# TensorE in the order of the program's text from attention on, and P's key blocks transposed two ahead, in a hybrid encoder block

## The chip, the cores and the metric

The kernel is one launch on one core of a Trainium2 chip. The time is the device time of that launch in microseconds (us). The engines go by the names of the profile: PE (TensorE; PEld are its weight loads), DVE (VectorE), ACT (ScalarE), POOL (GpSimd), SP (it issues the DMAs here). Each engine works through a list of its own, in the order in which the built program has it; engines wait for one another by semaphores.

## The reference

One layer on x of 4096 tokens by 1024 channels, in float32:

```python
mod = c @ w_ada + b_ada;  shift, scale, gate = split(mod, 3)
h = rms_norm(x, norm_g) * (1 + scale) + shift
q, k, v, u, z = split(h @ w_in)              # 512, 512, 512, 512, 1024 columns
q, k = rms_norm per head of 64, with q_norm_g, k_norm_g
A = attention of 8 heads: each chunk of 64 tokens sees itself and the 8 chunks to its left,
    with a clipped relative bias, softmax in float32
Pl = trailing means over 2, 4, 8, 16 tokens minus the token, a linear map per group, a scale per channel
x = x + gate * ((concat(A, Pl) * silu(z)) @ w_out)
```

## The kernel before

Every float32 product is made of three (or two) matmuls of rounded parts: an operand is split into a high part (a cast, on ACT) and the remainder (a subtraction, on DVE or POOL). The helper `split` (L109) does that.

A first stage (to some 557 us) makes h, the gate z, the pooled half and sums of the weights, and puts them into DRAM. The change touches what follows it.

**Attention** goes in two phases of four heads. A phase has 8 sections of 512 tokens, and a section has one unit per head, so there are 64 units, counted 0 to 63. Per unit `u` three lists of small steps are merged evenly by their place in the list (`merge`, L41): `s2_items` of unit u, `s1_items` of unit u+1, and `work`.

- `s1_items` (L679): for each of four query blocks, the scores (`sps`, L697 and L698) go into one PSUM buffer. DVE adds the bias and takes the minimum (L702); ACT makes the exponential (L715) into a tile `p`.
- `s2_items` (L734): for each of up to eight key blocks j, in the order of `js`, `tr(j)` transposes P on PE (`ptps`, L745), ACT copies the high part (`pth`, L751), DVE makes the remainder (`ptl`, L752), and `pv` multiplies with V (`ops`, L763 and L764). `LOOK` says how many key blocks `tr` is ahead of `pv`. The first key block of the list, j = -1, reads the tiles `p` of all four query blocks. `fin` copies the unit's output on ACT (`osum`, L778) and adds on DVE (L779); in every second unit POOL multiplies it twice (L781, L782).
- `work` holds most often one block of `proj_items` (L589): the projection of 128 tokens to q, k (512 columns, 24 matmuls) and v (256 columns, 24 matmuls; L599 to L601), six blocks ahead of the unit at the start. q and k are copied by ACT (`qkr`, L612), squared by POOL (`sq`, L614) and summed by DVE (L621). After every second block an inverse square root is made of small steps: two on DVE (L95, L96) and thirteen on POOL (L94, L99 to L102); then POOL multiplies both blocks' `qkr` (L630). The halves of h come by DMA and are split by ACT (`bhh`, L110) and POOL (`bhl`, L111), in three buffers each.
- Into `work` go also the transposes of q and k (`tq_items`, L646; PE's L651), four per section. They read the normalised `qkr` of four blocks. The first of a section stands in the unit after the one in which its last block is projected.

Units 26 and 27 have no projection of the first phase left; the second phase's weights are loaded there. Units 58 to 62 have output blocks instead (`o_items`, L519): 512 columns, `ps` from a pool of two buffers, L528 to L530, emptied by ACT or by DVE (L540). The last stage (`d_items`) is output blocks alone.

What sets the order before: the program is written in one order, but a scheduler with a timeline of its own puts each engine's instructions into the order in which it takes them to be ready:

```python
    with tile.TileContext(nc, schedule_with_timeline_sim=True) as tc:
```

Of the kernel before, what the change touches and what calls it, by code (L numbers as in the profile page):

```python
# [20 lines left out]
P = 128  # L21
# [7 lines left out]
HD = 64  # L29
HP = 4  # L30
WIN = 640
LOOK = 1
NPAIR = 16
EPS = 1e-6
NEG = 1e30
# [16 lines left out]
def block_kernel(ctx, tc, x, xT, par, crow, w_adaT, w_in, w_uT, bias, w_pool, w_out, rcnt, out):  # L52
# [423 lines left out]
                    load_wqkv(0, 1, lambda: a_stage(), nc.vector)  # L476


    op = ctx.enter_context(tc.tile_pool(name="b_qk", bufs=9))
    WO = {}  # L480

# [37 lines left out]
    def o_items(i):  # L519
        half, p = osteps[i]  # L520

        def one(k):
            if half == 0 and k == 0:
                XP[p] = (pp.tile([P, SG], F32, name="ps"), load_xr(p, 0))
            ps, xr = XP[p]
            a_, l_ = OH[i]
            wh, wl = WO[10 * half][k]
            nc.tensor.matmul(ps, a_[:, k, :], wh, start=half == 0 and k == 0, stop=False, skip_group_check=True)  # L528
            nc.tensor.matmul(ps, a_[:, k, :], wl, start=False, stop=False, skip_group_check=True)
            nc.tensor.matmul(ps, l_[:, k, :], wh, start=False, stop=k == 3, skip_group_check=True)  # L530
            if k == 3:
                OH.pop(i)
                o_load(i + 2)
                o_done(i)
                if half == 0:
                    t = op.tile([P, 512], F32, name="qkr")
                    nc.scalar.copy(t, ps)
                    nc.sync.dma_start(s1_d[p], t)
                else:
                    nc.vector.tensor_tensor(xr, ps, xr, op=ALU.add)  # L540
                    nc.sync.dma_start(out[p * P : (p + 1) * P, 0:512], xr)
                    XP.pop(p)

        return [lambda k=k: one(k) for k in range(4)]

    with ExitStack() as cb:
# [42 lines left out]
        def proj_items(ph, b, after=None):  # L589
# [3 lines left out]
            def chunk(c, k):  # L593
                if k == 0:
                    hold[c] = pp.tile([P, SG], F32, name="ps")
                ps = hold[c][:, 0:512] if c == 0 else hold[c][:, 0:256]
                a_, l_ = hq[(ph, b), k]
                wh, wl = WB[ph, c, k]
                nc.tensor.matmul(ps, a_, wh, start=k == 0, stop=False)  # L599
                nc.tensor.matmul(ps, a_, wl, start=False, stop=False)  # L600
                nc.tensor.matmul(ps, l_, wh, start=False, stop=k == KT - 1)  # L601
                if k == KT - 1:
                    if c == 0:
                        evac_qk(ps)
                    else:
                        evac_v(ps)
                if c == 1 and k in (3, 7) and after is not None:
                    load_h(*after, k // 4, nc.vector if ph == 0 and b < 5 else None)
# [37 lines left out]
        def tq_items(ph, sg):  # L646
            def tq(which, pair):
                ps = ptp.tile([P, SG], F32, name="ptps")
                c0 = which * 256 + pair * P
                for i in range(NB):  # L650
                    nc.tensor.transpose(  # L651
                        out=ps[:, i * P : (i + 1) * P], in_=QK[ph, sg * NB + i][:, c0 : c0 + P], identity=ident
                    )
                for e in range(2):
# [24 lines left out]
        def s1_items(ph, sg, h):  # L679
            def one(i):  # L680
# [13 lines left out]
                ks = ring[h]  # L694
                for pos, k0, n in parts:
                    o = ps[:, pos : pos + n]
                    nc.tensor.matmul(o, QS[ph, sg, h][:, qc], ks[:, k0 : k0 + n], start=True, stop=False)  # L697
                    nc.tensor.matmul(o, QL[ph, sg, h][:, qc], ks[:, k0 : k0 + n], start=False, stop=True)  # L698
                w0 = 0 if sg > 0 else 512 - i * P
                p_ = sp.tile([P, WIN], F32, name="p")  # L700
                mx = st.tile([P, 1], F32, name="mx")
# [32 lines left out]
        def s2_items(ph, sg, h):  # L734
# [5 lines left out]
            def tr(j):  # L740
                ilo, ihi = max(j, 0), min(j + 4, 3)
                ps = ptp.tile([P, SG], F32, name="ptps")
                for i in range(ilo, ihi + 1):
                    w = (j - i + 4) * P
                    nc.tensor.transpose(  # L745
                        out=ps[:, i * P : (i + 1) * P], in_=Pt[ph, sg, h, i][:, w : w + P], identity=ident
                    )
                r = slice(ilo * P, (ihi + 1) * P)
                a_ = wk.tile([P, SG], F32R, name="pth", bufs=3)
                l_ = wk.tile([P, SG], F32R, name="ptl", bufs=3)  # L750
                nc.scalar.copy(a_[:, r], ps[:, r])  # L751
                nc.vector.tensor_tensor(l_[:, r], ps[:, r], a_[:, r].bitcast(F32), op=ALU.subtract)  # L752
                pts[j] = (a_, l_, r)

            def pv(n):
# [4 lines left out]
                a_, l_, r = pts.pop(j)  # L760
                v = Vt[ph, sg * NB + j][:, pr, e, :]
                last = n == len(js) - 1
                nc.tensor.matmul(o[:, r], v, a_[:, r], start=n == 0, stop=False, skip_group_check=True)  # L763
                nc.tensor.matmul(o[:, r], v, l_[:, r], start=False, stop=last, skip_group_check=True)  # L764
                if last:
                    fin(o)

# [76 lines left out]
        def d_items(i):  # L844
            t, p = steps[i]

            def one(k):
# [12 lines left out]
                a_, l_ = DH[t, p]  # L860
                wh, wl = WO[11 if t == 0 else t][k]
                start = t in (1, 2) and k == 0
                nc.tensor.matmul(ps, a_[:, k, :], wh, start=start, stop=False, skip_group_check=True)
                nc.tensor.matmul(ps, a_[:, k, :], wl, start=False, stop=False, skip_group_check=True)  # L864
                nc.tensor.matmul(ps, l_[:, k, :], wh, start=False, stop=k == 3, skip_group_check=True)  # L865
                if k < 3:
                    return

# [156 lines left out]
```

## Time and profile before

| | us |
|---|---|
| three runs | 1914.45, 1915.05, 1915.29 (median 1915.05) |
| the profiled execution, its span | 1916.19, 1914.3 |
| PE, PEld busy | 1876.1 (98%), 1616.1 |
| DVE, ACT, POOL busy | 1198.1, 914.9, 697.7 |

A line of the profile names the source line, the engine, the operation, and the tiles as out<-in, with buffer numbers left out. "Idle before" is the idle time of the engine right before such instructions, and what ended most of it. The end of a matmul is modelled, and matmuls overlap, so the distance from one start to the next says what a matmul takes from PE.

### The profile page before, as it was taken

The page shows a single profiled execution, that of the slowest core. Times are in us where ns is not written, and L with a number is a line of the kernel's source. Part 1 is how long each engine was busy: PE and PEld are TensorE (multiplying, and loading weights), DVE is VectorE, ACT ScalarE, POOL GpSimd, SP SyncE. Part 2 cuts the span into 40 slices and gives each one's busy share as a digit, 9 for nine tenths or more (in the row PEclk, how much of TensorE's full clock was granted, in tenths as well). Part 3 has the DMA queues.
Part 4 walks back from the last instruction along what each step waited for, and adds up shares of the span by engine and source line. Part 5 has one row for each costly group of instructions (what it writes and reads, how often), then busy time and mean ns, then how long its engine had stood idle before and what let it go on. Part 6 is the DMA issues. An engine that isn't in the chain of part 4 may idle for free.

```text
span 1914.3 us, 29736 instructions
## 1 busy us (share of the span) xinstructions
PE 1876.1 (98%) x10284; PEld 1616.1 (84%) x10284; DVE 1198.1 (63%) x2424; ACT 914.9 (48%) x1951; POOL 697.7 (36%) x966
## 2 busy tenths in 40 slices
PE   8999999999999999999999999999999999989999
PEld 7888888888888888888887888988988888878887
DVE  8676666575544457656656665576566555478875
ACT  5422223332324457656657665576566666432221
POOL 0421355244135553444454564534444433200000
PEclk8999999999999999999999999999999999999999
DMA  9566466567222222221223222222212457686662
GB/s 376 192 198 198 151 216 213 185 200 258 75 100 73 72 67 67 65 69 53 60 83 111 78 85 75 69 61 67 67 62 67 181 185 230 234 297 221 208 205 78
DMA packets 196727, 265.63 MB, mean 139 GB/s; under 512 B 21984, under 2 KB 98272, under 8 KB 196576
## 3 DMA queue, kind: packets, MB, share of 16 engines
q1 hardware_dynamic: 196576, 263.73, 42.1%
q8 instruction: 81, 1.33, 0.3%
q14 instruction: 70, 0.57, 0.1%
HBM read 177.54 MB, written 77.74 MB: 133 GB/s over the span
## 4 chain that ended last, share of the span: by engine, by line
PE 90%; DVE 4%; ACT 2%; DMA 2%; issue 1%; SPq 0%; POOL 0%; ACTq 0%; DVEq 0%; POOLq 0%
PE ps L599 9%; PE ps L600 9%; PE ps L601 9%; PE ptps L745 6%; PE aps L330 5%; PE aps L332 5%; PE aps L331 5%; PE ps L330 4%; PE ps L331 4%; PE ps L332 4%; PE sps L697 3%; PE ops L764 3%; PE sps L698 3%; PE ops L763 3%; PE ptps L865 2%; PE ptps L864 2%
## 5 line engine op out<-in xcount | busy, mean ns | idle before, releaser
L599 PE MATMUL ps<-w,bhh 128*128 128x512 f32 (+1 forms) x1024 | 353.9, 346 | 0.8 <-ACT bhh L110 0.8
L600 PE MATMUL ps<-w,bhh 128*128 128x512 f32 (+1 forms) x1024 | 352.3, 344 | 0.4 <-DVE w L111 0.4
L601 PE MATMUL ps<-w,bhl 128*128 128x512 f32 (+1 forms) x1024 | 351.0, 343 | 0.0
L752 DVE TENSOR_TENSOR ptl<-ptps,pth 128x512 fp32r<-128x512 f32 x480 | 223.4, 485 | 157.3 <-ACT pth L751 153.0
L702 DVE CUSTOM_DVE_ANT_0 p<-sps,nb 128x640 f32<-128x640 f32 (+4 forms) x256 | 199.0, 777 | 127.6 <-PE sps L698 126.5
L751 ACT CAST pth<-ptps 128x512 fp32r<-128x512 f32 x480 | 192.5, 425 | 147.1 <-PE ptps L745 123.1
L111 POOL TENSOR_TENSOR bhl<-bhr,bhh 128x512 fp32r<-128x512 f32 x148 | 190.8, 1292 | 157.7 <-ACT bhh L110 123.4
L715 ACT ACTIVATE p<-p,mx 128x640 f32<-128x640 f32 (+4 forms) x256 | 204.5, 799 | 91.0 <-DVE mx L702 88.5
L745 PE MATMUL ptps<-ident,p 128*128 128x128 f32 x1200 | 215.3, 275 | 1.6 <-ACT p L715 1.4
L599 PEld LDWEIGHTS ps<-w,bhh 128*128 128x128 f32 x1024 | 194.2, 190 | 19.0 <-DVE v L111 1.1
L600 PEld LDWEIGHTS ps<-w,bhh 128*128 128x128 f32 x1024 | 194.1, 190 | 18.5 <-DVE w L111 1.1
L601 PEld LDWEIGHTS ps<-w,bhl 128*128 128x128 f32 x1024 | 194.1, 190 | 16.4
L763 PE MATMUL ops<-pth,v 128*128 128x512 f32 x480 | 162.3, 339 | 5.7 <-ACT pth L751 3.5
L745 PEld LDWEIGHTS ptps<-ident,p 128*128 128x128 f32 x1200 | 147.4, 140 | 21.0 <-ACT p L715 1.9
L697 PE MATMUL sps<-kr,qs 128*128 128x320 f32 (+2 forms) x480 | 154.5, 330 | 8.8 <-DVE mx L702 7.3
L764 PE MATMUL ops<-ptl,v 128*128 128x512 f32 x480 | 154.2, 331 | 2.9 <-DVE ptl L752 2.2
L614 POOL TENSOR_TENSOR sq<-qkr 128x512 f32<-128x512 f32 x64 | 66.6, 1041 | 247.1 <-ACT qkr L612 238.6
L331 PE MATMUL aps<-hlo,w 128*128 128x512 f32 x392 | 152.8, 390 | 0.0
L332 PE MATMUL aps<-hhi,w 128*128 128x512 f32 x392 | 152.8, 390 | 0.0
L330 PE MATMUL aps<-hhi,w 128*128 128x512 f32 x392 | 149.6, 392 | 0.0
L698 PE MATMUL sps<-kr,ql 128*128 128x320 f32 (+2 forms) x480 | 147.3, 317 | 0.0
L331 PE MATMUL ps<-hlo,w 128*128 128x512 f32 x376 | 146.6, 390 | 0.0
(202 smaller groups left out, 3932.0 us busy)
## 6 DMA issues: line engine op xcount, KB each, us to landing
bhr<-hT_d SPq DMA_DIRECT2D x128, 256.0 KB
xt<-in_x_dram SPq DMA_DIRECT2D x32, 512.0 KB
qkr<-in_x_dram SPq DMA_DIRECT2D x64, 256.0 KB
out_dram<-qkr SPq DMA_DIRECT2D x64, 256.0 KB
yv<-yT_d SPq DMA_DIRECT2D x61, 256.0 KB
xt<-in_xT_dram SPq DMA_DIRECT2D x28, 512.0 KB
hT_d<-xt SPq DMA_DIRECT2D x56, 256.0 KB
w<-wg_d SPq DMA_DIRECT2D x20, 512.0 KB
```

The costliest lines, as they stand in the source:

```text
L330: nc.tensor.matmul(ps, wh[:, cs], a_, start=k == 0, stop=False)
L331: nc.tensor.matmul(ps, wh[:, cs], l_, start=False, stop=False)
L332: nc.tensor.matmul(ps, wl[:, cs], a_, start=False, stop=k == KT - 1)
L599: nc.tensor.matmul(ps, a_, wh, start=k == 0, stop=False)
L600: nc.tensor.matmul(ps, a_, wl, start=False, stop=False)
L601: nc.tensor.matmul(ps, l_, wh, start=False, stop=k == KT - 1)
L697: nc.tensor.matmul(o, QS[ph, sg, h][:, qc], ks[:, k0 : k0 + n], start=True, stop=False)
L698: nc.tensor.matmul(o, QL[ph, sg, h][:, qc], ks[:, k0 : k0 + n], start=False, stop=True)
L745: nc.tensor.transpose(out=ps[:, i * P : (i + 1) * P], in_=Pt[ph, sg, h, i][:, w : w + P], identity=ident)
L752: nc.vector.tensor_tensor(l_[:, r], ps[:, r], a_[:, r].bitcast(F32), op=ALU.subtract)
L763: nc.tensor.matmul(o[:, r], v, a_[:, r], start=n == 0, stop=False, skip_group_check=True)
L764: nc.tensor.matmul(o[:, r], v, l_[:, r], start=False, stop=last, skip_group_check=True)
```

## The change

Three things change. `LOOK` goes from 1 to 2. `pth` and `ptl` have four buffers instead of three. And every matmul and transpose from attention on goes through `mm` or `turn_`, which tie it behind the instruction that stands before it on PE in the text: PE's list from there on is the order of the text, whatever the scheduler takes to be ready. The other engines' lists are still the scheduler's, which makes them for this order of PE. In the changed kernel all these matmuls bear the helper's lines, L481 and L484, and lines behind the helpers are 7 higher (L751 is L758, L778 is L785, L630 is L637).

```diff
-LOOK = 1
+LOOK = 2
...
+    def mm(*a, **kw):
+        tc.keep_in_program_order(nc.tensor.matmul(*a, **kw))
+
+    def turn_(**kw):
+        tc.keep_in_program_order(nc.tensor.transpose(**kw))
...
 # o_items, output blocks (three matmuls; the same in proj_items and d_items)
-            nc.tensor.matmul(ps, a_[:, k, :], wh, start=half == 0 and k == 0, stop=False, skip_group_check=True)
+            mm(ps, a_[:, k, :], wh, start=half == 0 and k == 0, stop=False, skip_group_check=True)
...
 # tq_items, transposes of q and k
-                    nc.tensor.transpose(
+                    turn_(
                         out=ps[:, i * P : (i + 1) * P], in_=QK[ph, sg * NB + i][:, c0 : c0 + P], identity=ident
...
 # s1_items, scores
-                    nc.tensor.matmul(o, QS[ph, sg, h][:, qc], ks[:, k0 : k0 + n], start=True, stop=False)
-                    nc.tensor.matmul(o, QL[ph, sg, h][:, qc], ks[:, k0 : k0 + n], start=False, stop=True)
+                    mm(o, QS[ph, sg, h][:, qc], ks[:, k0 : k0 + n], start=True, stop=False)
+                    mm(o, QL[ph, sg, h][:, qc], ks[:, k0 : k0 + n], start=False, stop=True)
...
 # s2_items, transposes of P and products
-                    nc.tensor.transpose(
+                    turn_(
                         out=ps[:, i * P : (i + 1) * P], in_=Pt[ph, sg, h, i][:, w : w + P], identity=ident
                     )
                 r = slice(ilo * P, (ihi + 1) * P)
-                a_ = wk.tile([P, SG], F32R, name="pth", bufs=3)
-                l_ = wk.tile([P, SG], F32R, name="ptl", bufs=3)
+                a_ = wk.tile([P, SG], F32R, name="pth", bufs=4)
+                l_ = wk.tile([P, SG], F32R, name="ptl", bufs=4)
...
-                nc.tensor.matmul(o[:, r], v, a_[:, r], start=n == 0, stop=False, skip_group_check=True)
-                nc.tensor.matmul(o[:, r], v, l_[:, r], start=False, stop=last, skip_group_check=True)
+                mm(o[:, r], v, a_[:, r], start=n == 0, stop=False, skip_group_check=True)
+                mm(o[:, r], v, l_[:, r], start=False, stop=last, skip_group_check=True)
```

**First place: ACT, entering unit 21.** p_9774 is the exponential of the unit's last query block, osum_9795 the copy of the finished unit's output, ops its products. Before:

```order
L751 CAST pth_9697<-ptps_9693 128x384
L751 CAST pth_9718<-ptps_9716 128x128
L751 CAST pth_9742<-ptps_9739 128x256
L715 ACTIVATE p_9774,ls_9636<-p_9774,mx_9775 128x640
L612 COPY qkr_10355<-ps_10257 128x512
L751 CAST pth_9762<-ptps_9760 128x128
L751 CAST pth_9817<-ptps_9812 128x512
L751 CAST pth_9830<-ptps_9825 128x512
L110 CAST bhh_10471<-bhr_10469 128x512
L715 ACTIVATE p_9842,ls_9845<-p_9842,mx_9843 128x640
L778 COPY osum_9795<-ops_9641 64x512
```

After the change:

```order
L722 ACTIVATE p_9730,ls_9636<-p_9730,mx_9731 128x640
L110 CAST bhh_9808<-bhr_9806 128x512
L758 CAST pth_9757<-ptps_9755 128x128
L785 COPY osum_9795<-ops_9658 64x512
L722 ACTIVATE p_9774,ls_9636<-p_9774,mx_9775 128x640
L110 CAST bhh_9970<-bhr_9968 128x512
L110 CAST v_9801<-ps_9716 128x2x64
L758 CAST pth_9817<-ptps_9812 128x512
L110 CAST v_9801<-ps_9716 128x2x64
```

The copy of the output stood seven rows behind the exponential; now it stands right ahead of it.

**Second place: PE, at the first transposes of q and k for section 6** (ptps out of ident and qkr; qkr_9904 is the last of the section's four blocks, projected into ps_9821). Before:

```order
L745 MATMUL ptps_10042<-ident_178,p_9842 128x128
L745 MATMUL ptps_10042<-ident_178,p_9884 128x128
L745 MATMUL ptps_10042<-ident_178,p_9951 128x128
L651 MATMUL ptps_10067<-ident_178,qkr_9259 128x128
L651 MATMUL ptps_10067<-ident_178,qkr_9483 128x128
L651 MATMUL ptps_10067<-ident_178,qkr_9704 128x128
L651 MATMUL ptps_10067<-ident_178,qkr_9904 128x128
L601 MATMUL ps_10584<-w_4611,bhl_10472 128x256
L599 MATMUL ps_10584<-w_4611,bhh_10471 128x256
L600 MATMUL ps_10584<-w_4612,bhh_10471 128x256
L601 MATMUL ps_10584<-w_4611,bhl_10472 128x256
L599 MATMUL ps_10693<-w_4445,bhh_10623 128x512
```

After the change:

```order
L481 MATMUL ps_10026<-w_4455,bhh_9970 128x512
L481 MATMUL ps_10026<-w_4456,bhh_9970 128x512
L481 MATMUL ps_10026<-w_4455,bhl_9971 128x512
L484 MATMUL ptps_10064<-ident_178,p_9842 128x128
L484 MATMUL ptps_10064<-ident_178,p_9884 128x128
L484 MATMUL ptps_10064<-ident_178,p_9951 128x128
L484 MATMUL ptps_10072<-ident_178,qkr_9259 128x128
L484 MATMUL ptps_10072<-ident_178,qkr_9487 128x128
L484 MATMUL ptps_10072<-ident_178,qkr_9704 128x128
L484 MATMUL ptps_10072<-ident_178,qkr_9904 128x128
L481 MATMUL ops_10085<-pth_10035,v_8264 128x512
L481 MATMUL ops_10085<-ptl_10036,v_8264 128x512
```

The last projection matmul into ps_9821 stood 382 rows ahead of the row that reads qkr_9904, and stands 74 rows ahead of it now. p_9995, the last query block's P of the unit, was transposed 15 rows after the q and k blocks; now that is done before them.

**Third place: POOL, between sq_9906 and the normalised qkr_9904** (sq_9906 stands eight rows ahead of this piece before, and eight ahead after the change). Before:

```order
L100 TENSOR_TENSOR rqw_9911<-rqw_9911,rqv_9909 128x16
L101 TENSOR_SCALAR rqw_9911<-rqw_9911 128x16
L102 TENSOR_TENSOR rqy_9910<-rqw_9911,rqy_9910 128x16
L99 TENSOR_TENSOR rqw_9911<-rqy_9910 128x16
L100 TENSOR_TENSOR rqw_9911<-rqw_9911,rqv_9909 128x16
L111 TENSOR_TENSOR bhl_10188<-bhr_10185,bhh_10187 128x512
L101 TENSOR_SCALAR rqw_9911<-rqw_9911 128x16
L102 TENSOR_TENSOR rqy_9910<-rqw_9911,rqy_9910 128x16
L630 TENSOR_TENSOR qkr_9704<-qkr_9704,rqy_9910 128x512
L630 TENSOR_TENSOR qkr_9904<-qkr_9904,rqy_9910 128x512
L781 TENSOR_TENSOR osum_9359<-osum_9359,gzb_9508 128x512
L782 TENSOR_TENSOR osum_9359<-osum_9359,rlx_9349 128x512
```

After the change:

```order
L99 TENSOR_TENSOR rqw_9911<-rqy_9910 128x16
L788 TENSOR_TENSOR osum_9795<-osum_9795,gzb_9944 128x512
L100 TENSOR_TENSOR rqw_9911<-rqw_9911,rqv_9909 128x16
L789 TENSOR_TENSOR osum_9795<-osum_9795,rlx_9785 128x512
L101 TENSOR_SCALAR rqw_9911<-rqw_9911 128x16
L102 TENSOR_TENSOR rqy_9910<-rqw_9911,rqy_9910 128x16
L99 TENSOR_TENSOR rqw_9911<-rqy_9910 128x16
L100 TENSOR_TENSOR rqw_9911<-rqw_9911,rqv_9909 128x16
L101 TENSOR_SCALAR rqw_9911<-rqw_9911 128x16
L102 TENSOR_TENSOR rqy_9910<-rqw_9911,rqy_9910 128x16
L637 TENSOR_TENSOR qkr_9704<-qkr_9704,rqy_9910 128x512
L637 TENSOR_TENSOR qkr_9904<-qkr_9904,rqy_9910 128x512
```

Between sq_9906 and the two qkr stood two bhl and the thirteen small steps; now two bhl, the small steps and the two multiplications of osum_9795, the output of the unit that has just been finished.

## Rows read from the trace of the kernel before

**Rows 1.** Stage window of attention: us, busy us of each engine, clock, DMA.

```profile
557.00:1640.00 1083.00, 1065.65 (x6602) 942.80 (x6601) 647.27 (x1517) 660.83 (x1507) 507.42 (x785) 1.00 0.29 91
```

**Rows 2.** Groups of PE, 557 to 1640: count, busy, mean ns, idle before.

```profile
L599 PE MATMUL ps<-w,bhh 128*128 128x512 f32 (+1 forms) x1024 | 353.9, 346 | 0.8 <-ACT bhh L110 0.8
...
L745 PE MATMUL ptps<-ident,p 128*128 128x128 f32 x1142 | 204.9, 275 | 0.4 <-ACT p L715 0.2
L763 PE MATMUL ops<-pth,v 128*128 128x512 f32 x456 | 154.5, 339 | 5.1 <-ACT pth L751 2.9 <-DVE osum L779 0.4 <-DVE rt L721 0.4
L697 PE MATMUL sps<-kr,qs 128*128 128x320 f32 (+2 forms) x464 | 149.6, 331 | 8.8 <-DVE mx L702 7.3 <-DVE kr L671 0.3
...
L528 PE MATMUL ps<-w,bhh 128*128 128x512 f32 x98 | 39.3, 404 | 0.0
L651 PE MATMUL ptps<-ident,qkr 128*128 128x128 f32 x256 | 38.9, 273 | 0.0
```

**Rows 3.** Timeline of PE: start, duration, line, tiles, columns.

```profile
1104.15 0.39 PE L601 MATMUL ps<-w,bhl 128*128 128x512 f32 x1
1104.38 0.28 PE L599 MATMUL ps<-w,bhh 128*128 128x256 f32 x1
...
1105.35 1.04 PE L745 MATMUL ptps<-ident,p 128*128 128x128 f32 x8
```

**Rows 4.** Timeline: one score, its bias on DVE, its exponential on ACT.

```profile
1433.61 0.34 PE L698 MATMUL sps<-kr,ql 128*128 128x384 f32 x1
...
1433.78 0.28 PE L697 MATMUL sps<-kr,qs 128*128 128x256 f32 x1
...
1433.90 0.28 PE L698 MATMUL sps<-kr,ql 128*128 128x256 f32 x1
...
1434.22 0.82 DVE L702 CUSTOM_DVE_ANT_0 p<-sps,nb 128x640 f32<-128x640 f32 x1 [1.23 <-PE sps L698]
...
1435.09 0.83 ACT L715 ACTIVATE p<-p,mx 128x640 f32<-128x640 f32 x1 [1.23 <-DVE mx L702]
```

**Rows 5.** Groups of ACT, 557 to 1640.

```profile
L110 ACT CAST bhh<-bhr 128x512 fp32r<-128x512 f32 x151 | 93.3, 619 | 68.6 <-PE ps L600 25.6 <-issue 15.2 <-POOL bhl L111 8.3
...
L778 ACT COPY osum<-ops 64x512 f32<-64x512 f32 x60 | 34.8, 580 | 22.0 <-PE ops L764 20.3 <-issue 0.4 <-POOL qkr L630 0.2
L110 ACT CAST v<-ps 128x128 fp32r<-128x128 f32 x128 | 33.0, 263 | 11.5 <-DVE v L111 10.9
```

**Rows 6.** Timeline of POOL: a normalisation of q and k.

```profile
1215.86 1.04 POOL L614 TENSOR_TENSOR sq<-qkr 128x512 f32<-128x512 f32 x1 [7.88 <-ACT qkr L612]
1216.86 1.30 POOL L781 TENSOR_TENSOR osum<-osum,gzb 128x512 f32<-128x512 f32 x1
1218.13 1.29 POOL L111 TENSOR_TENSOR bhl<-bhr,bhh 128x512 fp32r<-128x512 f32 x1
...
1222.43 0.22 POOL L99 TENSOR_TENSOR rqw<-rqy 128x16 f32<-128x16 f32 x1
1222.72 0.22 POOL L100 TENSOR_TENSOR rqw<-rqw,rqv 128x16 f32<-128x16 f32 x1
...
1227.14 2.04 POOL L630 TENSOR_TENSOR qkr<-qkr,rqy 128x512 f32<-128x512 f32 x2
```

**Rows 7.** Groups of DVE, 557 to 1640.

```profile
L540 DVE TENSOR_TENSOR qkr<-ps,qkr 128x512 f32<-128x512 f32 x11 | 7.6, 688 | 3.1 <-PE ps L530 3.0
```

**Rows 8.** Stage window behind a long wait of PE.

```profile
1708.00:1711.50 3.50, 3.50 (x10) 2.72 (x9) 3.14 (x6) 0.00 (x0) 0.00 (x0) 0.51 1.04 355
```

**Rows 9.** Timeline of PE there: matmuls of 512 columns.

```profile
1707.59 0.50 PE L863 MATMUL ps<-w,bhh 128*128 128x512 f32 x1 [2.35 <-DVE qkr L870]
...
1708.22 0.63 PE L865 MATMUL ps<-w,bhl 128*128 128x512 f32 x1
...
1711.57 0.40 PE L864 MATMUL ps<-w,bhh 128*128 128x512 f32 x1
```

More of the change, by code (lines that the diff above doesn't have):

```diff
@@ L527, in one @@
             wh, wl = WO[10 * half][k]
-            nc.tensor.matmul(ps, a_[:, k, :], wh, start=half == 0 and k == 0, stop=False, skip_group_check=True)
-            nc.tensor.matmul(ps, a_[:, k, :], wl, start=False, stop=False, skip_group_check=True)
-            nc.tensor.matmul(ps, l_[:, k, :], wh, start=False, stop=k == 3, skip_group_check=True)
+            mm(ps, a_[:, k, :], wh, start=half == 0 and k == 0, stop=False, skip_group_check=True)
+            mm(ps, a_[:, k, :], wl, start=False, stop=False, skip_group_check=True)
+            mm(ps, l_[:, k, :], wh, start=False, stop=k == 3, skip_group_check=True)
             if k == 3:
@@ L598, in chunk @@
                 wh, wl = WB[ph, c, k]
-                nc.tensor.matmul(ps, a_, wh, start=k == 0, stop=False)
-                nc.tensor.matmul(ps, a_, wl, start=False, stop=False)
-                nc.tensor.matmul(ps, l_, wh, start=False, stop=k == KT - 1)
+                mm(ps, a_, wh, start=k == 0, stop=False)
+                mm(ps, a_, wl, start=False, stop=False)
+                mm(ps, l_, wh, start=False, stop=k == KT - 1)
                 if k == KT - 1:
@@ L862, in one @@
                 start = t in (1, 2) and k == 0
-                nc.tensor.matmul(ps, a_[:, k, :], wh, start=start, stop=False, skip_group_check=True)
-                nc.tensor.matmul(ps, a_[:, k, :], wl, start=False, stop=False, skip_group_check=True)
-                nc.tensor.matmul(ps, l_[:, k, :], wh, start=False, stop=k == 3, skip_group_check=True)
+                mm(ps, a_[:, k, :], wh, start=start, stop=False, skip_group_check=True)
+                mm(ps, a_[:, k, :], wl, start=False, stop=False, skip_group_check=True)
+                mm(ps, l_[:, k, :], wh, start=False, stop=k == 3, skip_group_check=True)
                 if k < 3:
```

## The prediction

> **What bounds the kernel now.** I read the stage windows first, then the groups of PE, then pieces of the timeline. From 557 to 1640 us, the attention stage with most of the output blocks, PE is busy for 1065.65 of 1083 us at full granted clock, and DVE, ACT and POOL for 661 at most [rows 1]. So PE sets the time there, and a change can win only what PE waits, and lose by whatever new wait it gives PE.
>
> How much PE waits is not the 17 us of idle time, because a matmul that waits behind its weights' load is shown as a longer one. I count starts instead: the next matmul starts 0.23 us after one of 512 columns, a transpose takes 0.11 in a row of eight [rows 3]; 384 columns take 0.17 and 256 take 0.12 [rows 4]; 320 and 128 lie at 0.147 and 0.06 by their columns. L599 to L601 run 1024 times each, half at 512 and half at 256 columns: 534 us. L745 1142 and L651 256 transposes: 152 us. L763 and L764, 911 in all over four widths, mean 0.146: 133 us. L697 and L698, 928, mean 0.146: 136 us. L528 to L530, some 292: 67 us [rows 2]. Together 1022 us of 1083: PE waits 61 us in this stage. The largest shares named are the score matmul L697 behind DVE's L702 and the products L763 behind ACT's copies [rows 2]. L651, the transposes of the normalised q and k, wait 0.0 [rows 2], because the projections run far ahead of them: 382 rows of PE's order stand between a block's projection and the first transpose that reads it.
>
> **The change, part by part.** (a) One tile more of pth and ptl, and transposes two ahead: nothing is added in work, the same 10,256 matmuls. A product now stands at least 2 us of PE work behind its transposes, over a copy and a subtraction, so the L763 and L764 waits go. (b) Score matmuls stand evenly, some 3.3 us apart, against the 1.1 us that DVE needs to empty their one buffer [rows 4]: the L697 waits go. I take all 61 us as removed. What PE waits after 1640 I leave as it is. What is late next is what was moved to get there.
>
> (c) The strict order brings the reader close behind its producer at three places.
>
> *Entering a unit.* The first key block's transposes read all four query blocks' P, the last of which was scored late in the unit before. In the odd units with a projection block PE has, between the end of that score and the transpose that needs it, 2 products of 256 and 2 of 128 columns, 6 projection matmuls of 256 and 3 transposes: 1.41 us. In the even ones three matmuls of 512 more: 2.09. The chain needs: DVE starts 0.2 after the matmul, 0.82 for L702, 0.83 for the exponential L715 right behind it [rows 4], 0.14 to PE: 2.0 at best. But ACT's order now puts the copy of the finished unit's output (L778, 0.58) ahead of that exponential (first place of the order above), and its products end 0.72 after the score: 0.72+0.2+0.58 [rows 5]+0.83+0.14 = 2.45. Wait 1.0 in the odd, 0.35 in the even units. Where a bhh cast (0.62) stands there too, 1.65; where it and a v cast (0.26) stand behind the end of a projection block, 0.96+0.2+0.62+0.26+0.83+0.14 = 3.0, wait 0.9 [rows 5]. By ACT's order: 16 units at 1.0, 7 at 1.65, 11 at 0.35, 12 at 0.9, and 8 early units of each phase at 1.0 to 1.25: 51 us. If ACT's order cost nothing, 0.6 in the odd ones alone: 15 us. Each wait holds everything on PE behind the transpose, projections included.
>
> *The q and k transposes, 15 times (sections 1 to 15).* In the second place of the order above, PE's row for qkr_9904 comes after the projection of that block by 74 rows: 9 matmuls of 512, 28 of 256, 12 of 320, 2 of 384, 4 of 128 and 18 transposes; with the projection's last matmul 10.0 us, with the unit's 0.9 above 10.9. The producer is POOL. Its order in the third place, counted from that matmul's start: copy done at 1.0, sq 1.04, two bhl at 1.29, thirteen small steps at 0.29, two osum at 1.3, two qkr at 1.02 [rows 6]: 13.0. Two waits inside it: the first bhl's cast stands on ACT behind the copies of the running products (about 1.5), and the first small step's seed stands on DVE behind L702 of the last score (about 1.1); handovers 0.4. In all 16.1, so PE waits 5.2; times 15, 78 us. Bounds: with none of the four big foreign steps and no waits the chain is 8.6, and PE waits nothing; the chain in rows 6, with two osum, two bhl and a second sq inside, takes 13.3 from sq's start, 14.3 in all, a wait of 3.4; one foreign step more makes 17.5 and 6.6. I take 5.2, nearest to the list as it stands.
>
> *The output blocks (units 58 to 62).* Block p+1 begins in the buffer that DVE empties for block p-1 right before: 0.2+0.69 [rows 7]+0.1 = 1.0, less up to 0.5 of attention between: 0.8 at 15 places, 12 us. Between 0, if the merge always puts attention there, and 15.
>
> At the change of phase (units 26 and 27) no projection stands between, and POOL splits the next weights: PE is at the q and k transposes sooner and the chain is longer. I count that place at two more such waits, 11 us, between 0 and 20.
>
> (d) The clock. After a wait of 2.35 us near 1707 the granted clock was at 0.51, the lower level of 1.2 GHz, from 1708.0 to 1711.5 [rows 8]; eight matmuls of 512 columns took 3.35 us there instead of 1.8, a loss of 1.5 [rows 9]. The 5.2 us waits lie well above 2.35, the unit waits below: 15 times 1.5 is 23 us; 0 if the clock stays up, 46 if it stays down twice as long. The Trainium skill, TensorE: Matmul & The Clock Gate, section "Why this matters for your kernels", speaks against the change here: it says to leave no idle gaps between bursts of matmuls, since one brings the clock back down. By it the whole 23 us stand, without it the sum is 23 less; rows 8 and 9 agree with it.
>
> Sum, against the profiled execution's own 1916.2 us (span 1914.3): -61 +51 +78 +12 +11 +23 = +114, 2030. The median of the runs shown lies 1.1 below that execution: 2029.
>
> **The rivals.** *Short chain.* POOL's chain comes out as in rows 6, 3.4 us each (51), and the clock falls at every second one (12): -61+51+51+12+11+12, 1992. For it: most of the 2.6 of inner waits is my hand count. Against: the order of POOL and DVE is fixed, and lists them. *The strict order only removes waits (the other side).* If POOL had q and k ready within 10.9, as its own pieces (8.6) would allow, and the exponentials came as soon as their scores allow, what is left is 15 at the units and 12 at the outputs: -61+27, 1882. It decides where the new waits stay under 61. For it: POOL is busy in under half of the stage [rows 1]. Against: osum and bhl stand inside the chain in its order, and rows 6 show them being run there. *Nothing changes.* If PE's order were already nearly the text's, 1915; the 382 rows against 74 speak against it. *The waits feed each other*: the 5.2 us hold back the projection whose half of h the next chain's bhl waits for, and the clock stays down longer: 15 times 8 instead of 5.2, and 23 more, some 2095.
>
> **How the numbers follow.** Forecast 0.73, its own range 1995 to 2080; short chain 0.14; longer waits 0.06; only removed 0.05; nothing 0.02. The time is 2029. The range of 1985 to 2075 holds nearly all of the first case and about half of the second. Two runs of this kernel that differ by less than 0.2% (4 us) can't be told apart: faster 0.05, same 0.02, slower 0.93.
>
> **What would show it.** In the profile after, the transposes of q and k (ptps out of ident and qkr) should show 15 waits on POOL's qkr, some 5 us each, where before they had 0.0; the transposes of p some 50 waits on ACT's exponential of 0.3 to 1.7; L697's and L763's successors nearly none; PE's clock should fall for some microseconds behind each long wait. PE's idle time from its first projection to its last transposes should be near 170 us. I am wrong if the q and k waits are under 2 us, or if PE waits for something that I don't list, a transfer above all.

## The result, and the profile after

The changed kernel takes 2066.54 us (median of 4 runs, 2066.14 to 2066.98), the one before, run beside it, 1915.17: a ratio of 1.0789, 95% interval 1.0776 to 1.0803. It is slower by 151 us, where 114 were forecast.

The page's busy times and the row of the granted clock come first; in the second each digit is one fortieth of the span.

```profile
span 2065.2 us, 29785 instructions
...
PE 1919.7 (93%) x10284; PEld 1640.2 (79%) x10284; DVE 1216.2 (59%) x2424; ACT 921.1 (45%) x1951; POOL 697.4 (34%) x966
...
PEclk9999999999999999999998999999999999999999
```

The same stage as [rows 1], which now ends near 1790:

```profile
557.00:1790.00 1233.00, 1106.87 (x6607) 965.08 (x6605) 668.90 (x1525) 669.86 (x1516) 502.91 (x784) 0.96 0.26 81
```

Nearly the same matmuls (6607 against 6602) take 1233 us instead of 1083. PE is idle for 126 us of them instead of 17, and the mean clock is 0.96 instead of 1.00, although the page's digits hardly show it. DVE, ACT and POOL do the same work as before: nothing was added, something is waited for. The groups of PE say what (now all of line 481 or 484, so they are told apart by their tiles; these answer to L745, L697, L763 and L651 in [rows 2], where all widths of a line stand together; here each width has a row of its own):

```profile
L484 PE MATMUL ptps<-ident,p 128*128 128x128 f32 x1153 | 219.3, 282 | 37.4 <-ACT p L722 36.0 <-DVE ptl L759 1.3
...
L481 PE MATMUL sps<-kr,qs 128*128 128x320 f32 x242 | 75.1, 318 | 0.0
L481 PE MATMUL ops<-pth,v 128*128 128x512 f32 x115 | 52.9, 460 | 0.0
...
L484 PE MATMUL ptps<-ident,qkr 128*128 128x128 f32 x256 | 50.0, 298 | 76.7 <-POOL qkr L637 73.9 <-DVE ql L669 1.5 <-DVE ptl L759 1.3
```

The transposes of the normalised q and k wait 76.7 us, where [rows 2] had 0.0, and those of P 37.4 instead of 0.4. The scores of 320 columns and the products of 512 wait for nothing any more. But these products' mean has grown from 425 ns (the row of before, from 480 to 1720 us) to 460: some come first behind a wait, at the lower clock.

```profile
L763 PE MATMUL ops<-pth,v 128*128 128x512 f32 x120 | 51.1, 425 | 2.3 <-ACT pth L751 0.7 <-DVE osum L779 0.4 <-DVE rt L721 0.4
```

One such place in PE's timeline:

```profile
941.87 0.38 PE L484 MATMUL ptps<-ident,qkr 128*128 128x128 f32 x2
945.74 0.48 PE L484 MATMUL ptps<-ident,qkr 128*128 128x128 f32 x1 [3.49 <-POOL qkr L637]
946.74 0.48 PE L484 MATMUL ptps<-ident,qkr 128*128 128x128 f32 x1 [0.52 <-POOL qkr L637]
946.87 0.78 PE L481 MATMUL ops<-pth,v 128*128 128x512 f32 x1
...
950.86 0.63 PE L481 MATMUL ops<-pth,v 128*128 128x512 f32 x1
...
952.35 0.40 PE L481 MATMUL ps<-w,bhl 128*128 128x512 f32 x1
```

and the stretches in and behind it:

```profile
942.00:945.00 3.00, 0.25 (x3) 0.01 (x1) 0.99 (x2) 1.15 (x3) 2.51 (x8) 1.00 0.60 175
945.00:952.00 7.00, 5.74 (x15) 4.38 (x16) 1.93 (x3) 1.74 (x3) 1.69 (x2) 0.52 0.16 37
952.00:956.00 4.00, 4.00 (x25) 3.52 (x25) 1.39 (x3) 1.95 (x5) 0.00 (x0) 0.99 0.00 0
```

Two of the group's four transposes (one for each block) run, the third waits 3.7 us for POOL and the fourth 0.8 more. Then the granted clock stands at the lower of its two levels (1.2 GHz) for 6.8 us, and a matmul of 512 columns lasts 0.63 us instead of 0.40. What POOL does meanwhile (answers to [rows 6]):

```profile
932.28 1.04 POOL L621 TENSOR_TENSOR sq<-qkr 128x512 f32<-128x512 f32 x1 [8.62 <-ACT qkr L619]
934.88 1.29 POOL L111 TENSOR_TENSOR bhl<-bhr,bhh 128x512 fp32r<-128x512 f32 x1 [1.56 <-ACT bhh L110]
...
937.53 0.22 POOL L99 TENSOR_TENSOR rqw<-rqy 128x16 f32<-128x16 f32 x1 [1.07 <-DVE rqy L96]
937.89 1.27 POOL L111 TENSOR_TENSOR bhl<-bhr,bhh 128x512 fp32r<-128x512 f32 x1
...
940.20 1.30 POOL L788 TENSOR_TENSOR osum<-osum,gzb 128x512 f32<-128x512 f32 x1
...
941.64 1.27 POOL L789 TENSOR_TENSOR osum<-osum,rlx 128x512 f32<-128x512 f32 x1
...
944.64 2.04 POOL L637 TENSOR_TENSOR qkr<-qkr,rqy 128x512 f32<-128x512 f32 x2
```

Four large steps that have nothing to do with q and k stand inside the chain: two bhl, two osum, as its order lists them. The projection's last matmul started at 931.18, so the chain took 15.5 us. Inside it POOL stands idle twice: 1.56 us for ACT's cast of a bhh and 1.07 us for the seed of the root from DVE. And a unit's entry, ACT and PE in one timeline:

```profile
961.39 0.58 ACT L785 COPY osum<-ops 64x512 f32<-64x512 f32 x1 [1.26 <-POOL bhl L111]
...
961.56 0.49 PE L484 MATMUL ptps<-ident,p 128*128 128x128 f32 x3
961.88 0.83 ACT L722 ACTIVATE p<-p,mx 128x640 f32<-128x640 f32 x1
...
962.85 0.33 PE L484 MATMUL ptps<-ident,p 128*128 128x128 f32 x1 [0.80 <-ACT p L722]
```

DVE's maximum was there at 961.4; the exponential (L722) starts at 961.88, behind the copy of the finished unit (L785), and the fourth transpose waits for it.

To have all of it in one ledger I went through the starts of all matmuls in each trace (one profiled execution of each kernel, whose time can lie some us off the median): the time to the next start, less the usual spacing of that width (0.228 us for 512 columns, 0.175, 0.147, 0.120, 0.060 for the narrower ones, 0.109 for a transpose). Over 0.15 us it is a wait, put down to the matmul that came late; where the clock was down, the doubled spacing is put down to the clock (some 2 us of that column are a fall near 12 us, which every trace has). In us, with the median time (the experiments are below; "tail" are the blocks behind attention):

| kernel | q, k transposes | P transposes | scores, products | projections, outputs | tail | clock | time |
|---|---|---|---|---|---|---|---|
| before | 0 | 3.1 | 32.0 | 7.8 | 1.6 | 4.0 | 1915.2 |
| after | 83.6 | 46.9 | 5.1 | 12.3 | 7.5 | 43.3 | 2066.5 |
| look_only | 0.6 | 5.8 | 37.2 | 3.4 | 4.5 | 5.7 | 1922.8 |
| order_only | 61.2 | 34.0 | 27.1 | 15.2 | 3.3 | 25.1 | 2038.4 |
| turns_late | 14.5 | 53.6 | 8.2 | 12.9 | 6.2 | 11.4 | 1974.5 |
| fill_wait | 27.9 | 46.6 | 5.2 | 12.2 | 7.4 | 17.1 | 2041.8 |
| scores_early | 76.6 | 3.9 | 9.1 | 16.2 | 4.8 | 36.7 | 2015.1 |
| osum_dve | 61.9 | 46.4 | 6.3 | 14.7 | 5.4 | 34.1 | 2036.5 |
| ends_free | 51.5 | 42.6 | 6.3 | 1.8 | 5.1 | 28.2 | 2006.9 |
| part_pinned | 2.0 | 1.7 | 10.9 | 6.0 | 4.5 | 6.8 | 1901.1 |
| free_moves | 0.6 | 8.8 | 32.3 | 1.6 | 4.5 | 5.7 | 1920.7 |
| part_one_ahead | 0.3 | 10.3 | 19.5 | 6.3 | 2.9 | 5.2 | 1915.4 |

The columns of after add up to 198.7 and those of before to 48.5: 150.2 more, and the spans differ by 150.9. What is under 0.15 us adds up to some 30 us in either, so it is hardly a part of the change.

### The profile page after: what moved, and what is told of

Same layout as the page of the kernel before. It is cut to its first block, busy times and chain, and to the rows that moved or that the text cites. A ratio compares the mean times of both kernels' runs of the same rounds, so it can differ in the third digit from the quotient of the medians.

```text
span 2065.2 us, 29785 instructions
## 1 busy us (share of the span) xinstructions
PE 1919.7 (93%) x10284; PEld 1640.2 (79%) x10284; DVE 1216.2 (59%) x2424; ACT 921.1 (45%) x1951; POOL 697.4 (34%) x966
## 5 line engine op out<-in xcount | busy, mean ns | idle before, releaser
L481 PE MATMUL ps<-w,bhh 128*128 128x512 f32 (+1 forms) x2568 | 737.8, 371 | 10.0 <-DVE qkr L547 9.9
L481 PEld LDWEIGHTS ps<-w,bhh 128*128 128x128 f32 x2568 | 437.4, 195 | 49.2 <-DVE qkr L547 9.2
L481 PE MATMUL ps<-w,bhl 128*128 128x512 f32 (+1 forms) x1284 | 454.8, 354 | 0.0
L759 DVE TENSOR_TENSOR ptl<-ptps,pth 128x512 fp32r<-128x512 f32 x480 | 233.3, 489 | 197.0 <-ACT pth L758 191.2
L758 ACT CAST pth<-ptps 128x512 fp32r<-128x512 f32 x480 | 202.8, 423 | 234.6 <-PE ptps L484 231.2
L481 PEld LDWEIGHTS ps<-w,bhl 128*128 128x128 f32 x1284 | 246.5, 192 | 34.1
L484 PE MATMUL ptps<-ident,p 128*128 128x128 f32 x1200 | 227.5, 281 | 37.4 <-ACT p L722 36.0
L722 ACT ACTIVATE p<-p,mx 128x640 f32<-128x640 f32 (+4 forms) x256 | 204.1, 797 | 83.6 <-DVE mx L709 82.4
L484 PEld LDWEIGHTS ptps<-ident,p 128*128 128x128 f32 x1200 | 158.4, 144 | 85.3 <-ACT p L722 49.9
L481 PE MATMUL ops<-ptl,v 128*128 128x512 f32 x480 | 160.6, 335 | 0.7 <-DVE ptl L759 0.7
L481 PE MATMUL ops<-pth,v 128*128 128x512 f32 x480 | 156.9, 327 | 0.0
L481 PE MATMUL sps<-kr,qs 128*128 128x320 f32 (+2 forms) x480 | 150.4, 322 | 3.4 <-DVE mx L709 3.4
L481 PE MATMUL sps<-kr,ql 128*128 128x320 f32 (+2 forms) x480 | 147.0, 318 | 0.0
L332 PE MATMUL ps<-hhi,w 128*128 128x512 f32 x376 | 146.9, 391 | 0.0
L330 PE MATMUL ps<-hhi,w 128*128 128x512 f32 x376 | 146.3, 393 | 0.0
```

The lines of the kernel that those rows point to most:

```text
L330: nc.tensor.matmul(ps, wh[:, cs], a_, start=k == 0, stop=False)
L332: nc.tensor.matmul(ps, wl[:, cs], a_, start=False, stop=k == KT - 1)
L481: tc.keep_in_program_order(nc.tensor.matmul(*a, **kw))
L484: tc.keep_in_program_order(nc.tensor.transpose(**kw))
L722: nc.scalar.activation(p_[:, w0:WIN], p_[:, w0:WIN], AF.Exp, scale=-1.0, bias=mx, accum_out=ls)
```

## The experiments

The two parts of the change, each alone. First the look ahead, with the order free:

```
-LOOK = 1
+LOOK = 2
-a_ = wk.tile([P, SG], F32R, name="pth", bufs=3)      (ptl likewise)
+a_ = wk.tile([P, SG], F32R, name="pth", bufs=4)
```

> The kernel before with LOOK = 2 and four buffers of pth and ptl; TensorE's instructions stay free to be reordered. Theory: the loss lies in the strict order alone, and the second key block turned ahead can only take away part of the 15 us that products waited before, so 1900 to 1920 us, with no wait of the q and k transposes and no fall of the clock. Rival: turning two ahead costs by itself (one more P tile and one more PSUM tile are held, so scores or projections come later): 1930 us or more.

1922.79 us, ratio 1.0036 (1.0022 to 1.0049), just past the range on the slow side; the rival's 1930 was not reached. Hardly any q and k waits (0.6 us), and one fall of the clock that before has not, of 3.4 us at 1260.8, behind three short waits (0.4, 0.4 and 1.3 us). But the look ahead brought nothing either: the scores wait longer for DVE (first row; 7.3 us in all in before), and the products hardly less (12.7 against 14.9 by the ledger's count).

```profile
PE sps L697 <- DVE mx L702: 14.0, 23, 1.2
PE ops L763 <- ACT pth L751: 5.5, 6, 1.3
```

(Columns of this view: who waited for whom, us together, how many, the longest.) Then the order alone, the changed kernel with:

```
-LOOK = 2      (and four buffers of pth and ptl)
+LOOK = 1      (and three)
```

> The changed kernel with LOOK = 1 and three buffers of pth and ptl: the strict order alone. Theory: the 15 waits of the q and k transposes (some 4.6 us each) and the falls of the clock behind them are all there, and the products now stand one slot (about 2.1 us of TensorE work) behind their transposes instead of two, which the copy and the subtraction just fill: some products wait a few tenths, the unit entries wait a little less. 2055 to 2085 us. Rival: it is the second key block turned at a unit's entry that makes PE wait, then the time falls below 2020 us.

2038.44 us, ratio 1.0637 (1.0623 to 1.0652): 17 us under the forecast, and the rival's 2020 was not reached either. The strict order alone makes four fifths of the loss. The products wait, as expected (24 us by the ledger's count, of which the third row names 12.8); what I had not seen is that the q and k waits get shorter (61 us instead of 84), and the clock falls less often (25 instead of 43). Two things in the traces make them shorter. The products' waits stand ahead of the q and k transposes, so that PE comes to them 0.4 to 1.2 us later; and POOL's chain takes 14.4 us where it took 15.4, since it has one idle stretch of 1.5 us inside and not two. P's transposes wait 34 us instead of 47; what makes that difference was not tried by itself. So in the strict order the second key block takes away 22 us of waits of scores and products, and the time is 28 us longer all the same.

```profile
PE ptps L484 <- POOL qkr L637: 53.2, 32, 9.2
PE ptps L484 <- ACT p L722: 27.3, 30, 1.4
PE ops L481 <- DVE ptl L759: 12.8, 31, 1.5
```

Next, each of the new waits by itself. The q and k transposes later in the text:

```
-work.insert(min(len(work), 3 + 6 * n), f)
+work.insert(min(len(work), (9, 13)[n] if u % 4 == 2 else 3), f)
```

> The changed kernel with the first two groups of q and k transposes of a section put 6 and 4 items later in their unit (at the items 9 and 13 instead of 3 and 9), some 5.5 us of TensorE work. Theory: POOL's chain takes 14.3 to 15.5 us whatever PE does, so the 15 waits of 4.6 us go (about 70 us) and the clock no longer falls there (about 38): 2066 - 108, 1945 to 1975 us. The unit entries keep their 0.5 to 1.5 us waits and the clock stays at its upper level behind them. Rival: POOL's chain is itself paced by PE (its bhl steps wait for a half of h whose projection stands behind the wait), so it comes later too and about half of the waits stay: 2005 us or more. Second rival: the next unit's first scores then wait for qs and kr, and what was won is lost there: 1990 us or more.

1974.48 us, ratio 1.0305 (1.0291 to 1.0319): 92 us gone, of them 69 of q and k waits and 32 of the clock, at the range's end. POOL's chain takes 14.4 to 15.5 us as in the changed kernel (more only at the change of phase, 18 to 21 us in both), so it isn't paced by PE's wait. The falls of the clock are gone with the waits, but for the change of phase, where a wait of 7.4 us stays; the unit entries kept their waits. P's transposes wait 7 us more than before: some now stand behind the turned q, whose PSUM tile DVE has to empty for them (second row):

```profile
PE ptps L484 <- ACT p L722: 32.0, 55, 0.9
PE ptps L484 <- DVE ql L669: 12.2, 13, 1.5
PE ptps L484 <- POOL qkr L637: 11.3, 8, 7.4
```

Whether the clock falls because of the wait, or on its own, was asked by filling the wait with matmuls whose results are overwritten:

```
+if which == 0 and pair == 0 and (ph, sg) != (0, 0):
+    wh, _ = WB[ph, 0, 0]
+    for _ in range(16):
+        mm(ps, wh[:, 0:P], wh, start=True, stop=True)
 for i in range(NB):
     turn_(
```

> The changed kernel with 16 matmuls of 512 columns more (3.7 us, results overwritten) in front of the first q transposes of each section: 240 matmuls of work more, put into the time in which PE waits for POOL. It tells the clock from the wait. Theory: the granted clock falls because PE stands idle for 3.7 us and more. With the filler the idle time there is under 1 us except at the change of phase, the falls go, and although PE does 55 us more of work the time falls by some 36 us, to 2020 to 2040 us. Rival: the falls come from something else than the idle time (a period, or the load of the other engines): then they stay, and the time stays at 2066 us or rises.

2041.78 us, ratio 1.0654 (1.0639 to 1.0668), 2 us past the range: 240 matmuls more, and 24.8 us less time. The wait shrank by 55.7, which is the filler's own time (240 times 0.229 is 55), and 26.2 of clock came back. The first row below is the filler, and the two stretches around it are both at the full clock:

```profile
932.71 3.94 PE L481 MATMUL ptps<-w 128*128 128x512 f32 x16
936.48 0.55 PE L484 MATMUL ptps<-ident,qkr 128*128 128x128 f32 x3
937.70 0.33 PE L484 MATMUL ptps<-ident,qkr 128*128 128x128 f32 x1 [0.67 <-POOL qkr L637]
```

```profile
930.00:937.00 7.00, 7.00 (x37) 5.58 (x36) 3.53 (x7) 2.94 (x7) 6.26 (x16) 1.00 0.39 116
...
938.00:945.00 7.00, 7.00 (x42) 6.07 (x41) 3.32 (x6) 4.18 (x8) 0.37 (x1) 1.00 0.16 37
```

Most of what stays of the clock is at the change of phase, where waits of 5.6 and 3.2 us were left. It is shown, then, that the falls behind these waits follow the idle time and cost time of their own. The Trainium skill, "TensorE: Matmul & The Clock Gate", section "Why this matters for your kernels", says to leave no long idle gaps between bursts of matmuls; these rows agree, at 1.7 us for each of the 15 filled waits.

The scores earlier, for the units' entries:

```
-items.append(((i + 0.5) / len(l), n, i, f))
+items.append(((i + 0.5) / len(l) - (lead if n == 1 else 0), n, i, f))
-merge(s2_items(*units[u]), s1, work)
+merge(s2_items(*units[u]), s1, work, lead=0.12)
```

> The changed kernel with the scores of the next unit 0.12 of a unit (about 2 us of TensorE work) earlier in the text; nothing else. Theory: the first transposes of P wait 0.5 to 1.5 us at the units' entries (47 us together) because the last score is only 1.4 to 2.1 us of work ahead of them; with 2 us more between them nearly all of it goes, and since these waits never let the clock fall, nothing more: 2066 - 40, 2018 to 2038 us. The waits on POOL's qkr stay at about 84 us with their falls of the clock. Rival: ACT runs that exponential late because of what stands ahead of it in its order, so an earlier score does not help: 2050 us or more. Second rival: the scores then wait for their one buffer or for q and k: 2050 us or more, with waits on DVE's mx.

2015.09 us, ratio 1.0521 (1.0506 to 1.0537), 51 us gone where 28 to 48 were expected: 43.0 at P's transposes, as expected, and 7 each from the q and k waits and the clock, which were not: POOL's chain is some 1 us shorter here too (14.3 to 14.7 us in most sections), with less idle time inside. No wait on ACT's p is left among the larger ones, and that on POOL stays:

```profile
PE ptps L484 <- POOL qkr L637: 66.2, 32, 7.5
...
PE ptps L484 <- DVE ptl L759: 4.3, 4, 1.7
```

POOL's chain, by taking the two osum multiplications out of it:

```
-nc.gpsimd.tensor_tensor(Ot[pr], Ot[pr], hold["g"], op=ALU.mult)     (and rlb[pr])
+nc.vector.tensor_tensor(Ot[pr], Ot[pr], hold["g"], op=ALU.mult)
```

> The changed kernel with the two osum multiplications of a finished pair of heads on DVE instead of POOL. Theory: POOL's chain from the projection to the normalised k is the list of its steps, and two osum of 1.28 us stand inside it, so it gets 2.5 us shorter, the 15 waits of 4.6 us fall to about 2.1 (-37 us), and most of the falls of the clock go with them (-20 to -35): 1995 to 2025 us. Rival: the chain is long because of the handovers with ACT and DVE (the cast of bhh, the seed of the root), not because of foreign steps: it stays at 14 to 15 us and so does the time, 2055 us or more. Second rival: the 64 steps on DVE (0.6 us each) delay the exponentials and the products, and unit entries get as much longer: above 2035 us.

2036.47 us, ratio 1.0633 (1.0617 to 1.0648): 30 us gone, less than the 41 to 71 expected. The chain got shorter, but by 1.5 us (13.0 to 14.0), not 2.5: POOL's remaining steps became slower beside DVE's. Three rows of the two engines show it:

```profile
934.50 0.71 DVE L788 TENSOR_TENSOR osum<-osum,gzb 128x512 f32<-128x512 f32 x1
...
936.48 1.37 DVE L789 TENSOR_TENSOR osum<-osum,rlx 128x512 f32<-128x512 f32 x1
```

```profile
936.26 2.49 POOL L637 TENSOR_TENSOR qkr<-qkr,rqy 128x512 f32<-128x512 f32 x2
```

The chain is the list of its steps with the two idle stretches (1.56 and 1.07 us again), so the theory holds for the larger part of it and the rival, the handovers, for 2.6 us; the unit entries stayed at 46.4 us, so the second rival's reason does not hold, though its time does.

The ends of the stage, freed:

```
+m = nc.tensor.matmul(*a, **kw)
+if PIN[0]:
+    tc.keep_in_program_order(m)
...
+PIN[0] = 2 <= u < 25 or 32 <= u < 58
```

> The changed kernel with the order of the text kept only for the units 2 to 24 and 32 to 57; units 0 and 1, the change of phase (25 to 31), the output blocks (58 on) and the tail are free as before. Theory: the strict order costs at these places what the trace shows there: about 9 us in the first units, 24 at the change of phase with its falls of the clock, 12 at the output blocks and 9 at the tail's first block, together some 50, of which the order of before costs 15 to 20 itself: 2025 to 2040 us. The 12 or so waits on POOL's qkr in the pinned stretches stay. Rival: those waits are only put off (the borders between pinned and free stretches wait instead): 2055 us or more.

2006.89 us, ratio 1.0475 (1.046 to 1.0491): 60 us gone, 18 more than the range held. The output blocks' waits fall from 12.3 to 1.8, as expected, and the first units, the change of phase and the last section give back 32 of q and k waits and 15 of clock. The tail's waits stay (5.1; its first is the third row), and the kernel with the look ahead alone has them too (4.5): they aren't the strict order's, and what brings them was not tried by itself.

```profile
PE ptps L488 <- POOL qkr L643: 46.4, 22, 4.3
PE ptps L488 <- ACT p L728: 32.3, 49, 1.6
PE ptps L483 <- ACT bhh L110: 4.0, 1, 4.0
```

All three edits in one (with the lead and the free ends as above):

```
-work.insert(min(len(work), 3 + 6 * n), f)
+work.insert(min(len(work), (10, 14)[n] if u % 4 == 2 else 3), f)
```

> All of it at once, as a version that might beat both: the order of the text kept in units 2 to 24 and 32 to 57 only, the scores 0.12 of a unit earlier, the first two groups of q and k transposes at the items 10 and 14 of their unit instead of 3 and 9, two key blocks turned ahead. Theory: each of the three costs of the strict order is gone, and its gain (the 32 us that scores and products waited before) is left, less some 10 to 15 us of waits that stay: 1885 to 1905 us against 1916. Rival: with the room taken out, the orders of ACT, DVE and POOL, which are made anew, give other waits of the same size, as a kernel that is 98% busy has no room: 1912 us or more.

1901.10 us, ratio 0.9927 (0.9913 to 0.9941): 0.7% under before, a small gain but clear of the noise, and 8% under the changed kernel. The stage at its length here:

```profile
557.00:1620.00 1063.00, 1051.23 (x6587) 935.91 (x6586) 660.31 (x1522) 672.36 (x1509) 503.72 (x783) 1.00 0.29 91
```

```profile
PE ops L483 <- DVE ptl L765: 2.9, 11, 0.3
...
PE ptps L488 <- POOL qkr L643: 1.6, 2, 1.0
PE sps L483 <- DVE mx L715: 1.4, 4, 0.7
```

Its scores and products wait 10.9 us against 32.0 in before: that is the gain the order had to give. Two controls remain. The first has the same moves without the order kept (what is taken out of part_pinned):

```
-if PIN[0]:
-    tc.keep_in_program_order(m)
```

> The kernel before with the moves of the fastest version but no order kept: two key blocks ahead with four buffers, scores 0.12 of a unit earlier, q and k transposes at the items 10 and 14. It tells whether that version's gain comes from the moves or from the order kept. Theory: the gain is the order's: where TensorE's instructions are free they run as the planner puts them, the scores again close behind one another and behind DVE, and the text's places hardly count: 1912 to 1928 us, as with the look ahead alone (1922.8), with 20 to 25 us of waits of the scores. Rival: the moves themselves bring it: 1905 us or less.

1920.74 us, ratio 1.0028 (1.0017 to 1.0039): with a free order the same moves bring nothing, and scores and products wait 32.3 us, as in before. So the gain needs the order kept, and the order needs the moves: without them it only lost time. The second has all of part_pinned but the look ahead:

```
-LOOK = 2      (and four buffers of pth and ptl)
+LOOK = 1      (and three)
```

> The fastest version with one key block turned ahead and three buffers instead of two and four. It tells what turning two ahead is worth once nothing else of the strict order is in the way. Theory: a product then has one slot (2.1 us) in front of it for a copy of 0.42, a subtraction of 0.49 and their queues, and waits a few tenths in about half of the key blocks, as in the strict order alone (24 us of waits of the products against 1): 1912 to 1925 us, 10 to 25 over the fastest version. Rival: turning two ahead costs as it did in both other pairs (7 us free, 28 us in the strict order), since a unit's entry then waits for less: 1900 us or less.

1915.41 us, ratio 0.9995 (0.9987 to 1.0004): 14 us over the fastest version. The second key block ahead, which cost 7 us with a free order and 28 in the strict one, is worth 14 here, once nothing else is in its way:

```profile
PE ops L483 <- DVE ptl L765: 7.7, 17, 0.7
PE ptps L488 <- DVE ptl L765: 7.2, 10, 0.7
```

## Why the prediction was right, term by term

The time of 2066.5 us lies inside the stated range, 37 us above the forecast. The mechanism and the sign held: the strict order takes PE's room away at the q and k transposes, the unit entries and the output blocks, and the sum of that is far more than the waits it removes. Against the ledger's differences:

- *Removed waits*, -61: measured -27 (scores and products 32.0 to 5.1). This is the mis-sized term. The count of starts took everything over the usual spacings as a wait; of its 61 us 34 are waits over 0.15 us, and 27 are smaller excesses, which stand in both traces. The waits over 0.15 would have been the bound. (The matmuls are 10284 on both pages, not 10,256.)
- *q and k transposes*, +78 and +11 at the change of phase: measured +83.6. Ten of the 15 waits are 4.4 to 4.7 us (5.2 forecast), three 5.3 to 5.4, and the two at the change of phase 9.7 and 7.6; section 0, which had no term, waits 3.3. The chain takes 14.4 to 15.5 us away from the change of phase (16.1 forecast), and its list of steps is the one that was read from POOL's order. The two inner waits came nearly as forecast (1.56 and 1.07 us for 1.5 and 1.1); the handovers counted beside them and the small steps were too high. turns_late shows that the place makes the wait, osum_dve that the foreign steps are part of the chain.
- *Unit entries*, +51: measured +43.8, mostly between 0.5 and 1.5 as forecast; scores_early takes them away.
- *Output blocks*, +12: measured +4.5 in the ledger against before, which already waited 7.8 there and at the stage's end; 12.3 in all, and ends_free takes away 10.5.
- *Clock*, +23: measured +39. The waits were rightly put above the bound at which the trace of before showed a fall, but [rows 8] was one fall of 3.4 us; of the 18 behind 600 us in after, before the last instructions, eleven lasted 6.8 and one 13.7. That is near the 46 us that the prediction gave for a clock that stays down twice as long: the part of its rival of 2095 us that lies in the clock came nearly true; the longer waits of that rival did not come. fill_wait shows that it is a cost of its own.
- *The tail*, 0: measured +6, a wait of 3.6 us for a transfer into the tiles that attention frees, and a fall of the clock behind it. I had left what comes after 1640 as it was. PE waits for ACT's cast, and that for DVE's step, which a transfer held up:

```profile
PE ptps L481 <- ACT bhh L110: 3.6, 1, 3.6
```

```profile
1845.15 0.69 DVE L835 TENSOR_TENSOR yv<-yv,yp 128x512 f32<-128x512 f32 x1 [1.37 <-DMA yp<-yT_d]
```

The sum of the forecast was 37 us short: 34 from the removed waits, 16 from the clock, 6 from the tail, less some 20 on the other three. That these errors partly cancel is luck.

Of the two signs of being wrong, the first did not come: the q and k waits are above 2 us. The second came in small: the tail's wait for a transfer was not on the list, at 6 of the 151 us. Of what was to show the mechanism, the waits came as described (55 of P's transposes wait for ACT's exponential, 1.3 us at most); PE's idle time did not, 126 us from 557 to 1790 where 170 were forecast, though the time was longer than forecast. Of the rivals, the one on the other side (1882) was not made by this change, but its mechanism exists: part_pinned reaches 1901 with it, by giving the q and k transposes and the scores their room and by leaving the ends free.

## What to carry to other kernels

Before an order is fixed, count for each reader the work between it and its producer in that order against the producer's chain, the foreign steps on the producer's engine included: here 11 us against 15 made 15 waits. In this kernel a strict order and a longer look ahead were worth something only where every reader stood far enough behind: the same two edits cost 151 us, or gave 14 with two things moved in the text and the ends left free. And a wait that PE cannot fill can be dearer than it is long: behind the waits of 3.7 us and more the clock fell, behind the single waits at the units' entries (1.5 us at most) it did not.

## What was not expected of the hardware

A DVE step with two inputs in SBUF and POOL's steps there slow each other down. In osum_dve the second osum step takes 1.37 us on DVE while POOL normalises, and the first, a moment earlier, 0.71; POOL's pair takes 2.49 instead of 2.04; ten of the 64 osum steps on DVE meet POOL's pair in this way, all at 1.37. The Trainium skill, "SBUF — State Buffer", section "SBUF: two separate sides", says that a DVE step with two inputs in SBUF and a GpSimd step that reads SBUF take turns for a shared port, each for a whole instruction; the rows agree: 1.37 is 0.71 and some 0.7 of waiting. So a step that is taken from POOL to shorten its chain is not free if it lands beside that chain on DVE.

The length of a wait does not tell how long the clock stays down, nor does a single wait's length always tell whether it falls (look_only's fall at 1260.8 came behind three short ones). At 945 us PE waited 3.7 and 0.8 us, near 1020 it waited 3.8 and 0.9. Behind the first the clock stood at 1.2 GHz for 6.8 us (the stretch from 945 to 952 further up), behind the second for 3.4 (stretches of after; the granted clock is the third number from the end):

```profile
1020.40:1023.80 3.40, 2.88 (x9) 2.29 (x10) 0.90 (x2) 1.37 (x2) 0.47 (x1) 0.50 0.14 33
1023.80:1027.20 3.40, 3.40 (x19) 2.95 (x19) 1.82 (x4) 0.79 (x2) 0.00 (x0) 1.00 0.21 49
```
